# Layer 2's output projection: another order of features, tiles and PSUM banks

## The chip, the cores and the metric

The kernel runs on one core of a Trainium2 chip. The metric is the device time of one execution in microseconds. Three runs of the kernel before gave 1513.44 us in the median (1511.74 to 1513.91). The profile comes from one further execution.

## The reference, cut to what matters

A two-layer block with 512 latent tokens and 256 context tokens of width 1024. Each layer normalizes and modulates, mixes tokens in four branches of 256 features each, projects the 1024 mixed features with `w_out`, adds the result to x under a gate, normalizes again, and runs a convolutional FFN. In layer 2 only the latent tokens go on.

```python
def token_mixer(h_lat, h_ctx, ...):
    ya = gla_mixer(...)                       # gated linear attention, readout times silu(r)
    y = concatenate([ya, pool_mixer(zb), sgu_mixer(zc), conv_module(zd)]) @ w_out
...
x = layer_norm(ALPHA * x + m[2] * y, post_ln_w[l, 0], post_ln_b[l, 0])
h = modulate(x, m[3], m[4])
f = conv_ffn(h, ffn_w_up[l], ffn_conv_w[l], ffn_w_down[l])
x = layer_norm(ALPHA * x + m[5] * f, post_ln_w[l, 1], post_ln_b[l, 1])
```

## The kernel before, in words

All products are kept near fp32 accuracy by splitting each operand into a rounded part and a rest: `hi`/`lo` for weights, `hl`/`ll` for the latent tokens' features. `mm3` (lines 181 to 189) issues three matmuls per product: hi by hi, lo by hi, hi by lo. Line 133 is the subtraction that makes every rest (`lo`, `wl`, `ll`), on GpSimd or VectorE.

`mixers(l)` computes the four branches. At its end each of the eight feature blocks of 128 features is copied into `hl[k]` on ScalarE (line 865) and its rest into `ll[k]` (line 866, on VectorE for odd k, on GpSimd for even k), in the order `KORD`. Blocks 0 and 1 are the attention readout (`kT`, `qT`), 2 and 3 the pooled branch (`zs`), 4 and 5 the gated unit (`sy`, the tiles `cy`), 6 and 7 the convolution (`acc`).

What comes just before, in layer 2: the attention readout multiplies by the gate r on GpSimd (line 823), transposes on TensorE into a PSUM tile `yaT` (828), and ScalarE copies out with a scale (831). The convolution branch transposes its result into `cT` (799), normalizes it into `yn` (205 to 209), transposes back (805) and applies silu (810 to 813). The gated unit multiplies into a PSUM tile `s` (842), VectorE takes that out with bias and scale (846), and multiplies by the gelu of u (853); the gelu (499) reads the two columns `fl` that come last.

`out_proj` (lines 869 to 898) multiplies the blocks by `w_out`: each of four token tiles of 128 has two PSUM banks of 512 columns, y0 and y1. `w_out` comes in eight loads of 512 KB on SP's queue; the first two blocks of `KORD` get the weight buffers `hi`/`lo` that are free early, the other six lie in a pool of their own (`wh`, `wl`; line 882 and 133). Then `post_ln` (gate product 388, sum with the old x 389) and `norms` (two layer norms, lines 391 to 416) follow for a group of tiles, and `to_hT` (transposes `xT` 359, scale 365 and 367, copies 369) writes the new `hl`/`ll`. The constants of the norm (423, 424), the old x (384) and the gate rows `g` (435) are loaded into a pool whose memory the mixers' pools had. `ffn_up` then makes the first four FFN columns in two token halves, with the PSUM tiles `ul` in the banks 2, 3, 0, 5.

PSUM banks are handed out by rings, lists of bank numbers taken in turn (`rings`, `bank`). A bank is given on when every reader of its last tile is done. `stagger(ks, grp, n)` sets the loop order: all tiles of the group together over all but the last n blocks, then tile by tile over the last n.

The order in which an engine takes its instructions is not the program order: a planner, which simulates the timeline as the kernel is built, sorts each engine's queue by readiness and program order. On the chip each queue is taken in the order so fixed.

```python
def stagger(ks, grp, n):
    ks = list(ks)
    if ks[:-n]:
        yield ks[:-n], grp
    for t in grp:
        yield ks[-n:], (t,)
```

Of the kernel before, what the change touches and what calls it, by code (L numbers as in the profile page):

```python
# [13 lines left out]
ALU = mybir.AluOpType  # L14
# [5 lines left out]
KT = 8  # L20
# [30 lines left out]

CO, NCONST = offsets(CONSTS)
MO, NMIX = offsets(MIXW)
KORD = (0, 1, 6, 7, 2, 3, 4, 5)
PAIRS = ((0, 1), (3, 4), (2, 5))


# [1 line left out]
def kernel(  # L59
# [23 lines left out]
    V, S, G, PE = nc.vector, nc.scalar, nc.gpsimd, nc.tensor  # L83
# [11 lines left out]
    def rings(**kw):  # L95
        for n, r in kw.items():
            ring[n] = [r, 0]
# [344 lines left out]
# [8 lines that stand above are left out]
    def mixers(l, ms=None, pre=()):  # L450
        full = l == 0
# [214 lines left out]
        for p in range(2):  # L666
            V.scalar_tensor_tensor(out=sgb[:, p], in0=pt[:, p * 128:(p + 1) * 128], scalar=M["sgu_lnb"][:, p:p + 1],
                                   in1=M["sgu_b"][:, p * 128:(p + 1) * 128], op0=ALU.mult, op1=ALU.add)
# [27 lines left out]
        for t in order_t:  # L696
            po = bank("o", "sm")
            for c in range(2):
# [3 lines left out]
                for d in range(2):  # L702
                    i_s = st_of[d, ch]
                    if i_s == 0:
# [3 lines left out]
                                    in1=C["hm"].unsqueeze(2).to_broadcast([128, 4, 64]), op=ALU.mult)  # L708
# [60 lines left out]
        r_ = mx.tile([128, NT, 256], F32, name="r")  # L769
# [6 lines left out]
                V.scalar_tensor_tensor(out=r_[:, t], in0=r_[:, t], scalar=1.0, in1=pb[t][:, 0:256],  # L776
                                       op0=ALU.add, op1=ALU.mult)

        rings(**({"big": [2, 3], "sc": [4, 5]} if full else {"big": [4, 5], "sc": [0, 1]}))

        normalize([vg[:, t] for t in range(nt)], [vg[:, t] for t in range(nt)], "sgu", mx)

# [33 lines left out]
        for t0 in order_t[::2]:  # L816
            rs = rstd(ss[:, t0:t0 + 2].rearrange("p a b -> p (a b)"), 8, "rsg", 1.0 / 64.0, mx)
            yr = mx.tile([128, 2, 256], F32, tag="yr", name="yr")
            for i in range(2):
                V.tensor_tensor(out=yr[:, i].rearrange("p (h e) -> p h e", h=4),  # L820
                                in0=o_[t0 + i].rearrange("p (h e) -> p h e", h=4),
                                in1=rs[:, 4 * i:4 * i + 4].unsqueeze(2).to_broadcast([128, 4, 64]), op=ALU.mult)
            G.tensor_tensor(out=yr, in0=yr, in1=r_[:, t0:t0 + 2], op=ALU.mult)
            pt = bank("yaT", "sm")
            for k in range(2):
                for i in range(2):
                    o = k * 256 + i * 128
                    PE.transpose(pt[:, o:o + 128], yr[:, i, k * 128:(k + 1) * 128], ident)
            for k in range(2):
                ya = (kT, qT)[k][:, t0 * 128:(t0 + 2) * 128]  # L830
                S.activation(out=ya, in_=pt[:, k * 256:(k + 1) * 256], func=AF.Copy, scale=half[:, 0, k:k + 1])
# [25 lines left out]
        ys = [(kT, 0, LAT), (qT, 0, LAT), (zs[0], ZPAD, zo), (zs[1], ZPAD, zo), (sy[0], 0, LAT), (sy[1], 0, LAT),  # L857
              (yc[0], 0, CCTX), (yc[1], 0, CCTX)]
        for t0, n in spans:
            for k in KORD:  # L860
                y, o0, o1 = ys[k]
                o = o1 if t0 else o0
                src = y[:, o:o + n * 128]
                hi, lo = hcol(k, t0, n)
                S.activation(out=hi, in_=src, func=AF.Copy)
                sub_lo(V if k % 2 else G, lo, src, hi)
        es.close()

    def out_proj(l, groups, pb):
        with tc.tile_pool(name=f"ln1_{l}", bufs=2) as work, \  # L870
                tc.tile_pool(name=f"wo{l}", bufs=1, side="right") as wres:
            rings(sm=[6, 7] if l else [0, 1])
            ws = {}
            for i, k in enumerate(KORD):
                src = w_out[l, k * 128:(k + 1) * 128, :]
                if i < 2:
                    ws[k] = load_w(src, D)
                    continue
                st = load_st(src, D)
                hi = wres.tile([128, D], F32R, name=f"wh{k}")  # L880
                lo = wres.tile([128, D], F32R, name=f"wl{k}")
                S.activation(out=hi, in_=st, func=AF.Copy)
                sub_lo(V if k % 2 else G, lo, st, hi)
                ws[k] = (hi, lo)
            w, b = ln_consts(l, 0, work)
            gates = gate_get(l, 0, work)
            for grp in groups:
                ps = {t: (bank("y0", pb[t][0]), bank("y1", pb[t][1])) for t in grp}
                for ks, tiles in stagger(KORD, grp, KT):
                    for k in ks:  # L890
                        hi, lo = ws[k]
                        for t in tiles:
                            xh, xl = hcol(k, t)
                            for h in range(2):
                                s = slice(h * 512, (h + 1) * 512)
                                mm3(ps[t][h], hi[:, s], lo[:, s], xh, xl, k == KORD[0], k == KORD[-1], False)
                for _ in post_ln(l, 0, grp, ps, work, gates, w, b, lambda t: src_x(l, t), modT[l, 1]):
                    pass
# [233 lines left out]
    for l in range(DEPTH):  # L1132
# [3 lines left out]
        if l == 0:  # L1136
            out_proj(l, [(0, 1), (4, 5), (2,), (3,)], {0: (2, 3), 1: (4, 5), 4: (6, 7), 5: (2, 3), 2: (4, 5), 3: (6, 7)})
        else:
            out_proj(l, [(0, 1), (2,), (3,)], [(1, 4), (2, 3), (0, 5), (1, 4)])
        with tc.tile_pool(name=f"gT{l}", bufs=1, side="right") as gp, ExitStack() as late:  # L1140
            gT = [gp.tile([128, TOK if l == 0 else LAT], F32, name=f"gT{i}") for i in range(NF)]
            with ExitStack() as es:
# [151 lines left out]
```

## Time and profile before

| what | value |
|---|---|
| median of three runs | 1513.44 us (1511.74 to 1513.91) |
| profiled execution, its own time | 1510.28 us |
| span of its instructions | 1508.5 us |
| TensorE (PE) busy | 1448.1 us, 96% |
| VectorE (DVE) busy | 1172.2 us, 78% |
| ScalarE (ACT) busy | 544.7 us, 36% |
| GpSimd (POOL) busy | 830.0 us, 55% |
| mean granted TensorE clock | 0.989 |

Times in the rows are microseconds from the start of the span; a row with x8 stands for eight instructions run together. The time in brackets is how long the engine sat idle before, with the instruction that ended the wait. Matmuls overlap with their successors, so the distance of two starts, not the duration of one, is the pace. The execution profiled was 3.16 us faster than the median.

### The profile page before, as it was taken

The page shows a single profiled execution, that of the slowest core. Times are in us where ns is not written, and L with a number is a line of the kernel's source. Part 1 is how long each engine was busy: PE and PEld are TensorE (multiplying, and loading weights), DVE is VectorE, ACT ScalarE, POOL GpSimd, SP SyncE. Part 2 cuts the span into 40 slices and gives each one's busy share as a digit, 9 for nine tenths or more (in the row PEclk, how much of TensorE's full clock was granted, in tenths as well). Part 3 has the DMA queues.
Part 4 walks back from the last instruction along what each step waited for, and adds up shares of the span by engine and source line. Part 5 has one row for each costly group of instructions (what it writes and reads, how often), then busy time and mean ns, then how long its engine had stood idle before and what let it go on. Part 6 is the DMA issues. An engine that isn't in the chain of part 4 may idle for free.

```text
span 1508.5 us, 22357 instructions
## 1 busy us (share of the span) xinstructions
PE 1448.1 (96%) x8389; PEld 1185.7 (79%) x8389; DVE 1172.2 (78%) x1896; ACT 544.7 (36%) x936; POOL 830.0 (55%) x695
## 2 busy tenths in 40 slices
PE   6999999999999989999999989999899999999997
PEld 5776567788788878888888767986678888888875
DVE  6429987796988888787533699798687999889596
ACT  5443224245333322323211234254426454443121
POOL 2432635455665655543445597215466888777374
PEclk9999999999999999999999999999999999999999
DMA  9544410634877666521432366632162333333431
GB/s 377 195 165 158 140 54 15 228 135 159 313 266 240 239 215 216 178 70 56 165 100 85 116 204 239 209 125 71 58 234 72 98 98 98 98 98 93 173 112 56
DMA packets 67196, 227.11 MB, mean 151 GB/s; under 512 B 7289, under 2 KB 7945, under 8 KB 66065
## 3 DMA queue, kind: packets, MB, share of 16 engines
q1 hardware_dynamic: 67088, 225.69, 44.3%
q8 instruction: 66, 1.08, 0.3%
q14 instruction: 42, 0.34, 0.1%
HBM read 198.12 MB, written 27.55 MB: 150 GB/s over the span
## 4 chain that ended last, share of the span: by engine, by line
PE 62%; DVE 14%; DMA 12%; POOL 6%; issue 4%; ACT 2%; SPq 1%; POOLq 0%; DVEq 0%; ACTq 0%
PE ul L183 8%; PE ul L184 8%; PE ul L185 8%; PE f L187 5%; PE f L188 5%; PE f L189 5%; DMA ms<-in_wmodT 3%; POOL lo L133 2%; PE fl L183 2%; PE fl L185 2%; PE fl L184 2%; DVE acc L730 2%; DMA wl_f<-ms 2%; POOL ms L133 2%; PE tk L187 2%
## 5 line engine op out<-in xcount | busy, mean ns | idle before, releaser
L133 POOL TENSOR_TENSOR lo<-st,hi 128x512 fp32r<-128x512 f32 x300 | 412.2, 1397 | 228.0 <-ACT hi L147 175.1
L945 DVE SCALAR_TENSOR_TENSOR acc<-ul,cvw,acc 128x441 f32<-128x441 f32 (+2 forms) x660 | 437.1, 690 | 43.4 <-ACT acc L916 20.6
L147 ACT ACTIVATE hi<-st 128x1024 fp32r<-128x1024 f32 (+1 forms) x176 | 184.6, 1051 | 366.1 <-PE f L189 164.1
L184 PE MATMUL ul<-ll,hi 128*128 128x512 f32 (+1 forms) x768 | 286.4, 374 | 0.7 <-POOL ll L133 0.4
L183 PE MATMUL ul<-hl,hi 128*128 128x512 f32 (+1 forms) x768 | 284.8, 375 | 1.1 <-ACT hl L369 1.1
L185 PE MATMUL ul<-hl,lo 128*128 128x512 f32 (+1 forms) x768 | 285.4, 373 | 0.0
L187 PE MATMUL f<-hi,gh 128*128 128x512 f32 x440 | 171.8, 395 | 1.2 <-DVE gh L1007 1.2
L188 PE MATMUL f<-lo,gh 128*128 128x512 f32 x440 | 172.6, 394 | 0.0
L189 PE MATMUL f<-hi,gl 128*128 128x512 f32 x440 | 164.3, 396 | 6.4 <-POOL gl L133 5.3
L183 PEld LDWEIGHTS ul<-hl,hi 128*128 128x128 f32 x768 | 144.5, 190 | 28.3 <-issue 2.5
L185 PEld LDWEIGHTS ul<-hl,lo 128*128 128x128 f32 x768 | 145.5, 189 | 25.7 <-issue 0.4
L184 PEld LDWEIGHTS ul<-ll,hi 128*128 128x128 f32 x768 | 145.7, 190 | 24.6 <-POOL ll L133 0.7
L949 POOL TENSOR_TENSOR gT<-acc 128x768 f32<-128x768 f32 (+1 forms) x44 | 69.8, 1586 | 96.1 <-ACT acc L948 76.0
L730 DVE SCALAR_TENSOR_TENSOR acc<-cy,cmw,acc 128x798 f32<-128x798 f32 (+1 forms) x120 | 117.0, 1016 | 0.8
L183 PE MATMUL uc<-hc,hi 128*128 128x256 f32 x352 | 100.6, 286 | 6.5 <-DVE acc L945 6.4
L189 PEld LDWEIGHTS f<-hi,gl 128*128 128x128 f32 x440 | 82.6, 189 | 27.1 <-POOL gl L133 7.7
L185 PE MATMUL uc<-hc,lo 128*128 128x256 f32 x352 | 100.4, 285 | 0.0
L184 PE MATMUL uc<-lc,hi 128*128 128x256 f32 x352 | 100.4, 285 | 0.0
L187 PEld LDWEIGHTS f<-hi,gh 128*128 128x128 f32 x440 | 83.3, 189 | 20.6 <-issue 1.8
L188 PEld LDWEIGHTS f<-lo,gh 128*128 128x128 f32 x440 | 83.2, 189 | 18.3
L1007 DVE CAST gh<-gT 128x256 fp32r<-128x256 f32 x66 | 37.4, 572 | 64.9 <-PE f L188 64.9
L133 POOL TENSOR_TENSOR gl<-gT,gh 128x256 fp32r<-128x256 f32 x66 | 54.8, 833 | 57.8 <-DVE gh L1007 50.7
(304 smaller groups left out, 2843.6 us busy)
## 6 DMA issues: line engine op xcount, KB each, us to landing
st<-in_w_up SPq DMA_DIRECT2D x88, 512.0 KB, 3.5
st<-in_w_down SPq DMA_DIRECT2D x66, 512.0 KB, 3.5
ms<-in_wmodR SPq DMA_DIRECT2D x48, 512.0 KB, 4.1
ms<-in_wmodT SPq DMA_DIRECT2D x32, 512.0 KB, 3.7
ms<-in_wmod SPq DMA_DIRECT2D x8, 1024.0 KB, 12.3
st<-in_w_out SPq DMA_DIRECT2D x16, 512.0 KB, 3.5
x<-z SPq DMA_DIRECT2D x16, 512.0 KB, 2.8
z<-x SPq DMA_DIRECT2D x14, 512.0 KB, 8.8
```

Source lines behind the costliest of these rows:

```text
L133: eng.tensor_tensor(out=lo, in0=src, in1=f(hi), op=ALU.subtract)
L147: S.activation(out=hi[:, :n], in_=st[:, :n], func=AF.Copy)
L183: PE.matmul(ps, wh, xh, start=first, stop=False)
L184: PE.matmul(ps, wh, xl, start=False, stop=False)
L185: PE.matmul(ps, wl, xh, start=False, stop=last)
L187: PE.matmul(ps, xh, wh, start=first, stop=False)
L188: PE.matmul(ps, xh, wl, start=False, stop=False)
L189: PE.matmul(ps, xl, wh, start=False, stop=last)
L730: V.scalar_tensor_tensor(out=acc[i][:, :cw], in0=src, scalar=wj, in1=acc[i][:, :cw], op0=ALU.mult, op1=ALU.add)
L945: V.scalar_tensor_tensor(out=d, in0=u, scalar=w, in1=d, op0=ALU.mult, op1=ALU.add)
L949: G.tensor_tensor(out=gT[i][:, :n], in0=ag[:, :n], in1=aa[:, :n], op=ALU.mult)
L1007: V.tensor_copy(out=gh, in_=src)
```

## The change

Only layer 2's order changes, but for one table that now has an entry per layer:

- The blocks are copied and multiplied in the order 2, 3, 4, 5, 6, 7, 0, 1 in layer 2 (layer 1 keeps 0, 1, 6, 7, 2, 3, 4, 5). So `w_out`'s blocks are loaded in that order too, and 2 and 3 get the early buffers.
- `stagger` gets 4 instead of 8 in layer 2: tiles 0 and 1 together over the first four blocks, then tile 0, then tile 1 over the last four.
- The tiles' banks in layer 2 become (2,3), (4,5), (0,1), (2,3) instead of (1,4), (2,3), (0,5), (1,4).
- Behind the last token projection of layer 2, the ring `sm` shrinks to banks 6 and 7 (it had 6, 7, 2, 3): the two `yaT` and the two `s` take 6, 7, 6, 7.
- The attention readout's gate product in layer 2 runs on VectorE instead of GpSimd.

```diff
--- before.py
+++ after.py
@@ -51,7 +51,7 @@
 
 CO, NCONST = offsets(CONSTS)
 MO, NMIX = offsets(MIXW)
-KORD = (0, 1, 6, 7, 2, 3, 4, 5)
+KORDS = ((0, 1, 6, 7, 2, 3, 4, 5), (2, 3, 4, 5, 6, 7, 0, 1))
 PAIRS = ((0, 1), (3, 4), (2, 5))
 
 
@@ -776,7 +776,7 @@
                 V.scalar_tensor_tensor(out=r_[:, t], in0=r_[:, t], scalar=1.0, in1=pb[t][:, 0:256],
                                        op0=ALU.add, op1=ALU.mult)
 
-        rings(**({"big": [2, 3], "sc": [4, 5]} if full else {"big": [4, 5], "sc": [0, 1]}))
+        rings(**({"big": [2, 3], "sc": [4, 5]} if full else {"big": [4, 5], "sc": [0, 1], "sm": [6, 7]}))
 
         normalize([vg[:, t] for t in range(nt)], [vg[:, t] for t in range(nt)], "sgu", mx)
 
@@ -820,7 +820,7 @@
                 V.tensor_tensor(out=yr[:, i].rearrange("p (h e) -> p h e", h=4),
                                 in0=o_[t0 + i].rearrange("p (h e) -> p h e", h=4),
                                 in1=rs[:, 4 * i:4 * i + 4].unsqueeze(2).to_broadcast([128, 4, 64]), op=ALU.mult)
-            G.tensor_tensor(out=yr, in0=yr, in1=r_[:, t0:t0 + 2], op=ALU.mult)
+            (G if full else V).tensor_tensor(out=yr, in0=yr, in1=r_[:, t0:t0 + 2], op=ALU.mult)
             pt = bank("yaT", "sm")
             for k in range(2):
                 for i in range(2):
@@ -857,7 +857,7 @@
         ys = [(kT, 0, LAT), (qT, 0, LAT), (zs[0], ZPAD, zo), (zs[1], ZPAD, zo), (sy[0], 0, LAT), (sy[1], 0, LAT),
               (yc[0], 0, CCTX), (yc[1], 0, CCTX)]
         for t0, n in spans:
-            for k in KORD:
+            for k in KORDS[l]:
                 y, o0, o1 = ys[k]
                 o = o1 if t0 else o0
                 src = y[:, o:o + n * 128]
@@ -870,7 +870,7 @@
         with tc.tile_pool(name=f"ln1_{l}", bufs=2) as work, \
                 tc.tile_pool(name=f"wo{l}", bufs=1, side="right") as wres:
             rings(sm=[6, 7] if l else [0, 1])
-            ws = {}
+            ws, KORD = {}, KORDS[l]
             for i, k in enumerate(KORD):
                 src = w_out[l, k * 128:(k + 1) * 128, :]
                 if i < 2:
@@ -886,7 +886,7 @@
             gates = gate_get(l, 0, work)
             for grp in groups:
                 ps = {t: (bank("y0", pb[t][0]), bank("y1", pb[t][1])) for t in grp}
-                for ks, tiles in stagger(KORD, grp, KT):
+                for ks, tiles in stagger(KORD, grp, 4 if l else KT):
                     for k in ks:
                         hi, lo = ws[k]
                         for t in tiles:
@@ -1136,7 +1136,7 @@
         if l == 0:
             out_proj(l, [(0, 1), (4, 5), (2,), (3,)], {0: (2, 3), 1: (4, 5), 4: (6, 7), 5: (2, 3), 2: (4, 5), 3: (6, 7)})
         else:
-            out_proj(l, [(0, 1), (2,), (3,)], [(1, 4), (2, 3), (0, 5), (1, 4)])
+            out_proj(l, [(0, 1), (2,), (3,)], [(2, 3), (4, 5), (0, 1), (2, 3)])
         with tc.tile_pool(name=f"gT{l}", bufs=1, side="right") as gp, ExitStack() as late:
             gT = [gp.tile([128, TOK if l == 0 else LAT], F32, name=f"gT{i}") for i in range(NF)]
             with ExitStack() as es:
```

## Rows read from the trace of the kernel before

**Rows 1.** Stretches: from:to, length, then busy us (xcount) per engine, clock, DMA share, GB/s

```profile
1077.00:1090.00 13.00, 8.86 (x41) 6.91 (x42) 11.42 (x18) 7.60 (x13) 8.57 (x6) 1.00 0.22 74
...
1101.66:1144.00 42.34, 40.32 (x227) 34.24 (x226) 39.01 (x80) 16.45 (x30) 27.21 (x30) 1.00 0.44 160
...
1128.00:1147.00 19.00, 15.64 (x119) 13.91 (x117) 16.52 (x41) 11.87 (x30) 10.24 (x16) 1.00 0.14 58
...
1147.00:1480.00 333.00, 331.92 (x1511) 276.53 (x1511) 293.25 (x416) 131.90 (x183) 248.25 (x194) 1.00 0.33 105
```

**Rows 2.** TensorE in order of time: start, us, operation, [idle before, releaser]

```profile
1067.04 1.10 PE L842 MATMUL s<-mw,vg 128*64 128x128 f32 x16
...
1077.19 0.66 PE L828 MATMUL yaT<-cst,yr 128*128 128x128 f32 x4 [0.42 <-POOL yr L823]
...
1079.89 0.50 PE L187 MATMUL y<-hi,hl 128*128 128x512 f32 x1 [2.05 <-ACT hl L865]
...
1081.84 0.60 PE L805 MATMUL cT<-cst,yn 128*128 128x128 f32 x4
...
1089.36 0.50 PE L187 MATMUL y<-wh,hl 128*128 128x512 f32 x1 [1.91 <-ACT hl L865]
...
1126.93 0.39 PE L188 MATMUL y<-wl,hl 128*128 128x512 f32 x1
...
1127.16 0.39 PE L189 MATMUL y<-wh,ll 128*128 128x512 f32 x1
```

**Rows 3.** TensorE in order of time, start of layer 2's FFN

```profile
1128.98 0.74 PE L183 MATMUL ul<-hl,hi 128*128 128x256 f32 x4 [0.78 <-ACT hl L369]
...
1146.91 0.74 PE L183 MATMUL ul<-hl,hi 128*128 128x256 f32 x4 [0.32 <-ACT hl L369]
```

**Rows 4.** Chain of waits, 1070 to 1160 us: start, us, what

```profile
1092.50 0.33 SPq L423
...
1092.88 6.68 DMA lnb<-in_post_b
```

**Rows 5.** VectorE in order of time, 1044 to 1160 us

```profile
1076.01 0.54 DVE L810 TENSOR_SCALAR acc<-cT,half 128x256 f32<-128x256 f32 x1 [1.44 <-PE cT L805]
...
1077.14 0.73 DVE L846 SCALAR_TENSOR_TENSOR cy<-s,mw,sgb 128x512 f32<-128x512 f32 x1
...
1080.38 1.00 DVE L209 TENSOR_SCALAR yn<-cT,bmv_cm,rs_cm 128x256 f32<-128x256 f32 x2 [0.59 <-POOL rs_cm L194]
...
1083.52 2.61 DVE L133 TENSOR_TENSOR wl<-st,wh 128x1024 fp32r<-128x1024 f32 x1 [0.29 <-ACT wh L882]
...
1086.05 2.59 DVE L813 SCALAR_TENSOR_TENSOR acc<-yn,acc 128x256 f32<-128x256 f32 x1
...
1091.66 0.69 DVE L133 TENSOR_TENSOR ll<-acc,hl 128x512 fp32r<-128x512 f32 x1 [0.70 <-ACT hl L865]
...
1101.66 1.36 DVE L388 TENSOR_TENSOR y<-y,g 128x512 f32<-128x512 f32 x2 [4.48 <-DMA g<-gates]
...
1115.61 0.69 DVE L216 BATCH_NORM_STATS2 bst_m<-z 128x6 f32<-128x512 f32 x1 [1.17 <-POOL z L405]
```

**Rows 6.** GpSimd in order of time, 1044 to 1160 us

```profile
1064.89 1.27 POOL L133 TENSOR_TENSOR ll<-z,hl 128x512 fp32r<-128x512 f32 x1 [6.42 <-ACT hl L865]
...
1075.86 1.27 POOL L823 TENSOR_TENSOR yr<-yr,r 128x512 f32<-128x512 f32 x1
```

**Rows 7.** ScalarE in order of time, 1044 to 1160 us

```profile
1074.46 0.58 ACT L499 ACTIVATE tmp<-fl 128x512 f32<-128x512 f32 x1
...
1078.25 0.47 ACT L831 ACTIVATE qT<-yaT,half 128x256 f32<-128x256 f32 x1
...
1081.47 2.95 ACT L882 ACTIVATE wh<-st 128x1024 fp32r<-128x1024 f32 x3 [0.59 <-DVE yn L209]
```

**Rows 8.** TensorE in order of time, 870 to 886 us

```profile
880.31 1.74 PE L189 MATMUL f<-hi,gl 128*128 128x512 f32 x4 [3.01 <-POOL gl L133]
```

**Rows 9.** Stretch behind that pause, columns as in the first group

```profile
880.30:884.00 3.70, 3.69 (x10) 2.91 (x11) 3.70 (x7) 0.00 (x0) 3.70 (x5) 0.56 0.97 343
```

## The prediction

> **What bounds the kernel now.** I read the stretches first. From 1147 us on, TensorE works 331.92 of 333.00 us [rows 1]: whatever layer 2's FFN starts earlier or later by goes straight into the total. The change sits just ahead of it, so the question is what sets that start. Next TensorE in order of time: behind the mixers it pauses 0.42 us for GpSimd's gated product, 2.05 us for the first `hl` copy and 1.91 us for the copy of convolution feature 6, then streams `y` matmuls 0.23 us apart until about 1127.4 [rows 2]. Pauses: 4.4 us. If TensorE alone set the end, that would be the gain.
>
> It does not. The chain of waits leaves TensorE at 1092.50 and goes through SP's load of the layer norm's constants [rows 4]. These loads have memory that the mixers' pool gives back, and they go out 0.15 us after the pool's last reader, the `ll` copy of feature 7, 1091.66 + 0.69 [rows 5]. Behind them come the old x and the gate rows `g`; VectorE sits 4.48 us until `g` lands and starts the first post norm at 1101.66 [rows 5]. From there to 1144 VectorE works 39.01 of 42.34 us [rows 1]: it is the bound of the four post norms. TensorE has slack behind it: 3.36 us idle between 1128 and 1147 [rows 1], and the second token half of the first FFN columns waits for the last `hl` copies until 1146.91 [rows 3]. So the path is: convolution branch, pool release at 1092.4, constants and gates by DMA, VectorE's post norms, FFN. TensorE's three pauses lie beside it.
>
> **The change part by part.**
>
> *Order 2,3,4,5,6,7,0,1, tiles 0 and 1 together over the first four, banks (2,3) and (4,5).* The work stays 192 `y` matmuls, some 44 us at 0.23. Pooled features 2 and 3 are ready early: their copies run from about 1064 (the `ll` of the first at 1064.89 [rows 6]), and their weights take the two early slots that 0 and 1 had, with the same eight 512 KB loads in the same places of SP's queue. Banks 4 and 5 fall free with the second gelu, 1074.46 + 0.58 [rows 7]. So 24 matmuls (two features, two tiles, two halves, three products), 5.6 us, can stand where TensorE now waits; features 4 and 5 give 24 more, whose weights cannot start before 1081.47 [rows 7]. Both long pauses should go: 4.0 us of TensorE. On the path this is worth nothing by itself, since the first post norm still waits for `g`. Tile 0 then needs 72 matmuls and the last weights; from 1077.4 (the end of `yaT`, less its 0.42 us pause) that is 1094, with the twelve to twenty-four of tile 2 that fill in 1097 to 1100, still before 1101.66. If that cover were gone, each later microsecond would count in full.
>
> *What tiles 2 and 3 give.* Their `y` ends about 4.4 us earlier, at 1123 instead of 1127.4. VectorE can then fill pauses of its chain with their evacuations: it idles 42.34 - 39.01 = 3.33 us in the stretch [rows 1], 1.17 of it in one wait for GpSimd's end of tile 0's norm [rows 5]. Bounds 0 and 3.3; I take the middle, 1.6, because some of these waits are short round trips to GpSimd that no other tile's work fits into. Tile 3's third feature also frees the early weight buffers sooner, so GpSimd's split of the third and fourth FFN weight comes earlier too; same work, another place.
>
> *`sm` banks 6 and 7.* The second `yaT` and the second `s` now both use bank 7. Today the second half of `s` stands in front of the conv transposes on TensorE and its evacuation L846 (0.73 us at 1077.14) in front of the conv statistics' end on VectorE [rows 5]. Afterwards `s` must wait until ScalarE has emptied `yaT`, now 1078.25 + 0.47 [rows 7]. If the planner lets the conv branch pass, L846 (0.73), the product behind it (about the 0.69 of the `ll` copy of the same shape [rows 5]) and half of the 1.10 us of sixteen `s` matmuls [rows 2] leave the path: up to 2.0 earlier. If L846 keeps its place, it waits for `s`: the product ends 1.9 earlier (below), so bank 7 is free at 1076.8, `s` ends at 1077.9, and with a hand-over it costs 1.2.
>
> *Gating on VectorE.* Twice a 1.27 us GpSimd product [rows 6] becomes a VectorE product of the size of that 0.69 us copy. The one that matters can run from 1074.6, inside VectorE's 1.44 us pause before 1076.01 [rows 5]; so nothing is paid, and `yaT` comes up to 1.9 us earlier (1077.13 against 1075.25). Without that cover it costs 0.7. A row warns here: a VectorE product beside GpSimd's work took 2.61 us at 1083.52, and a 128x256 one behind it 2.59 [rows 5]; at twice the 0.69 us it would still end at 1076.0, when the pause ends.
>
> Together these two move the pool release by between -1.2 (later) and +2.0; I take +1.0, nearer the gain, because VectorE takes its queue in the planner's order and the conv statistics stand earlier in the program than the wait of `s` ends.
>
> *Tile 3 in banks 2 and 3.* These are the FFN's first two `ul` banks; today they are tile 1's and long free. The first columns now wait for tile 3's evacuation. The columns in banks 0 and 5 can go meanwhile, and the evacuation must come anyway before tile 3's norm; cost 0, up to 1 if TensorE's queue has the blocked ones in front.
>
> *Sum.* 1.0 (release) + 1.6 (filled pauses) + 0 (rest) = 2.6 us, all carried through the FFN. Against the profiled execution, span 1508.5 in 1510.28, this gives 1507.7; that execution lies 3.2 under the median of 1513.44, so the median becomes **1510.8 us**.
>
> *The clock.* TensorE's pause before the FFN grows from 0.78 us [rows 3] to about 4. Once it paused 3.01 us [rows 8], and the next 3.70 us show a granted clock of 0.56, near the 1.2 GHz level, and ten matmuls [rows 9], which at 0.23 take 2.3: a loss of 1.4, inside the 3.36 of slack. The Trainium skill, "TensorE: Matmul & The Clock Gate", section "HAM oscillation — how this bites in real kernels", says that matmuls which come in short bursts between waits start cold again each time. The rows agree for one pause; no row here shows a series. By the row the sum stays; by the page the first `ul` matmuls, which come in bursts as the `hl` copies land, would all run at half rate, and the slack would be used up.
>
> **Rivals.**
>
> 1. *Given back whole.* The release stays at 1092.4 and the pauses of VectorE are round trips; TensorE's 4 us become a longer wait before 1129, perhaps with the slow clock in it. For it: VectorE is 92% busy from 1101.66 [rows 1]. Against: the conv branch has two movable items. Gain 0 to 0.6: 1513.1 (1512.8 to 1513.5).
> 2. *Larger.* The conv branch also gets in front of the weight split on VectorE: the 2.61 us at 1083.52 [rows 5] leave the path on top. For it: that order is the planner's and hangs on a microsecond. Against: the weights start at the same event, the last `yn`. 1510.8 - 2.6 = 1508.2 (1506 to 1509).
> 3. *Slower: `y` in front of the conv transposes.* TensorE takes its queue in order. The last `cT` transposes stand at 1081.84, today behind eight `y` matmuls [rows 2]. If more than (1081.84 - 1077.4) / 0.23 = 19 stand in front, each further one delays the conv branch, the release and all behind it by 0.23. With the 24 of features 2 and 3 and eight of feature 4 it is 32, thirteen too many: 3.0 us; with all of feature 4, 3.9. Less the 1.6 of filled pauses: 1.4 to 2.3 slower, **1515.3** (1514 to 1517.5, the upper end with the bank wait of L846). For it: `y` work is now ready 4 us before the transposes. Against: the transposes come first in the program, and the planner knows when they are ready.
>
> **How the numbers follow.** Forecast (1509 to 1512.8) 0.38; rival 1 0.20; rival 2 0.20; rival 3 0.22. Two in a thousand, 3.0 us, is about what a measurement here can tell: faster means under 1510.4, slower over 1516.5. Faster: rival 2 and somewhat under half of the forecast, 0.20 + 0.17 = 0.37. Slower: half of rival 3, 0.11. Same: the rest, 0.52. The range leaves out the lower end of rival 2 and the upper part of rival 3: 1507 to 1515.5.
>
> **What would show it.** Right: no pause over 0.5 us on TensorE between 1077 and the last `y`; `y` ending 4 us earlier; the SP load of L423 about 1 us earlier; L388's first start near 1100.7; a pause of some 4 us before the first `ul`; the first wait-free `ul` second half near 1144.3. Rival 3 shows as more than 19 `y` matmuls in front of the last four `cT` transposes. The prediction is wrong in its root if the first L388 waits for TensorE instead of `g`, or if the FFN's start follows the end of `y` rather than VectorE.

## Result, and the profile after

The change made the kernel slower: 1520.29 us in the median of five runs (1516.03 to 1521.96) against 1513.44 us for the kernel before (five runs, 1509.80 to 1513.91), 6.85 us between the medians. The ratio between the runs is 1.0053, with an interval of 1.0035 to 1.007, which is 8 us. The time lies outside the predicted range and on the other side of no change.

The profiled execution after took 1521.96 us, 11.7 more than the one before, and not all of that is the change. The same kernel's executions differ by some microseconds in layer 1, ahead of anything edited. I therefore count every time below from one event ahead of the change, the first gelu of `vg` on ScalarE, and call the start of the first full-width `ul` matmul of layer 2's FFN **F**. From F to the end of the span lie 349.4 to 349.6 us in the profiles of all 20 kernels told of here, so what the change does to the time is what it does to F. In order: start, us, operation. Before:

```profile
1049.02 0.38 ACT L773 ACTIVATE vg<-tk 128x256 f32<-128x256 f32 x1 [0.97 <-PE tk L189]
...
1158.95 0.40 PE L183 MATMUL ul<-hl,hi 128*128 128x512 f32 x1
```

After:

```profile
1053.50 0.38 ACT L773 ACTIVATE vg<-tk 128x256 f32<-128x256 f32 x1 [0.97 <-PE tk L189]
...
1170.66 0.40 PE L183 MATMUL ul<-hl,hi 128*128 128x512 f32 x1
```

F is 109.93 before and 117.16 after. So 4.48 us of the 11.7 lie ahead of the change, and 7.23 us are its own, in line with the timed 8.

**Where they were lost first: the release.** TensorE after, in order of time, around what answers to [rows 2] and [rows 3]:

```profile
1083.91 1.09 PE L842 MATMUL s<-mw,vg 128*64 128x128 f32 x16
1084.94 0.66 PE L828 MATMUL yaT<-cst,yr 128*128 128x128 f32 x4
1085.43 0.60 PE L805 MATMUL cT<-cst,yn 128*128 128x128 f32 x4
...
1087.36 1.09 PE L842 MATMUL s<-mw,vg 128*64 128x128 f32 x16
1089.66 0.50 PE L187 MATMUL y<-wh,hl 128*128 128x512 f32 x1 [1.22 <-ACT wh L882]
...
1092.61 0.50 PE L188 MATMUL y<-wl,hl 128*128 128x512 f32 x1 [1.52 <-POOL wl L133]
...
1132.32 0.44 PE L359 MATMUL xT<-cst,xh 128*128 128x128 f32 x2 [2.19 <-DVE xh L412]
...
1139.93 1.54 PE L359 MATMUL xT<-cst,xh 128*128 128x128 f32 x6 [7.17 <-DVE xh L412]
1142.28 1.22 PE L183 MATMUL ul<-hl,hi 128*128 128x256 f32 x4 [0.81 <-ACT hl L369]
```

Both `s` come late: the first starts at 30.41 (before 18.02), and the second stands behind the second `yaT`, whose bank 7 it takes over, and ends at 34.95 (before 27.74). ScalarE and SP after:

```profile
1086.00 0.47 ACT L831 ACTIVATE qT<-yaT,half 128x256 f32<-128x256 f32 x1
...
1087.85 0.63 ACT L865 ACTIVATE hl<-cy 128x512 fp32r<-128x512 f32 x1
1088.56 2.95 ACT L882 ACTIVATE wh<-st 128x1024 fp32r<-128x1024 f32 x3
...
1120.39 1.06 ACT L147 ACTIVATE hi<-st 128x1024 fp32r<-128x1024 f32 x1 [3.28 <-PE y L189]
```

```profile
1099.43 0.33 SPq L423 DMA_DIRECT2D lnw<-in_post_w  x1
```

SP's load of `lnw`, at 43.48 before [rows 4], goes out at 45.93. The release is 2.45 late. The conversion of the late `w_out` blocks starts 0.11 behind the end of the second `s`, at 35.06; before, it started behind the last `yn` ([rows 7], 1081.47), at 32.45. But ScalarE was busy with copies until 0.08 before it, and VectorE, which takes the last steps to the release, did not stand waiting for its result. What changed there is VectorE's order. VectorE before, beside [rows 5]:

```profile
1068.18 0.75 DVE L846 SCALAR_TENSOR_TENSOR cy<-s,mw,sgb 128x512 f32<-128x512 f32 x1
...
1078.73 0.66 DVE L853 TENSOR_TENSOR cy<-cy,tmp 128x512 f32<-128x512 f32 x1
```

and after:

```profile
1084.27 0.99 DVE L209 TENSOR_SCALAR yn<-cT,bmv_cm,rs_cm 128x256 f32<-128x256 f32 x2 [0.25 <-POOL rs_cm L194]
1085.18 0.74 DVE L846 SCALAR_TENSOR_TENSOR cy<-s,mw,sgb 128x512 f32<-128x512 f32 x1
...
1086.53 0.68 DVE L853 TENSOR_TENSOR cy<-cy,tmp 128x512 f32<-128x512 f32 x1
1087.54 1.36 DVE L133 TENSOR_TENSOR ll<-qT,hl 128x512 fp32r<-128x512 f32 x1 [0.33 <-ACT hl L865]
...
1090.71 0.73 DVE L846 SCALAR_TENSOR_TENSOR cy<-s,mw,sgb 128x512 f32<-128x512 f32 x1
1091.47 1.63 DVE L853 TENSOR_TENSOR cy<-cy,tmp 128x512 f32<-128x512 f32 x1
1093.03 3.42 DVE L133 TENSOR_TENSOR wl<-st,wh 128x1024 fp32r<-128x1024 f32 x1
...
1098.58 0.69 DVE L133 TENSOR_TENSOR ll<-acc,hl 128x512 fp32r<-128x512 f32 x1
```

The last `yn` itself ends at 31.76, earlier than before (32.36). But before, VectorE had emptied both `s` (L846) and made both products (L853) ahead of it; after, all four stand behind it, 3.78 us together, on the way to the last reader of the pool, the `ll` at 1098.58. From 1087.54 to there VectorE never pauses longer than 0.10 us. This is read from the order of one profile; what the edits do to it one by one is told below.

**Where they were lost next: GpSimd's queue.** VectorE after, answering to [rows 5]:

```profile
1082.98 0.69 DVE L823 TENSOR_TENSOR yr<-yr,r 128x512 f32<-128x512 f32 x1
...
1108.63 1.34 DVE L388 TENSOR_TENSOR y<-y,g 128x512 f32<-128x512 f32 x2 [2.67 <-DMA g<-gates]
...
1123.47 0.69 DVE L216 BATCH_NORM_STATS2 bst_m<-z 128x6 f32<-128x512 f32 x1 [1.18 <-POOL z L405]
...
1126.40 2.20 DVE L402 SCALAR_TENSOR_TENSOR z<-z,rs_p,lnb 128x832 f32<-128x832 f32 x1
...
1132.65 1.07 DVE L402 SCALAR_TENSOR_TENSOR z<-z,rs_p,lnb 128x832 f32<-128x832 f32 x1
...
1139.34 0.54 DVE L412 TENSOR_SCALAR xh<-z,bmv_m,rs_m 128x512 f32<-128x512 f32 x1
```

The first post norm still waits for `g`, and starts 2.49 late, as the release does. But tile 1's `xh` (1139.34) is at 85.84 instead of 77.51, 8.3 late. One reason is GpSimd, here before (`z` L405 is the end of a tile's post norm, `lo` the split of an FFN weight, `rs` a power that closes a statistic):

```profile
1108.50 5.05 POOL L133 TENSOR_TENSOR lo<-st,hi 128x512 fp32r<-128x512 f32 x4 [1.27 <-DMA st<-in_w_up]
...
1117.02 0.80 POOL L405 TENSOR_TENSOR z<-z,lnw 128x192 f32<-128x192 f32 x1 [0.94 <-ACT z L401]
1117.90 0.60 POOL L405 TENSOR_TENSOR z<-z,lnb 128x192 f32<-128x192 f32 x1
...
1119.91 5.22 POOL L133 TENSOR_TENSOR lo<-st,hi 128x512 fp32r<-128x512 f32 x4
```

and after:

```profile
1115.47 5.94 POOL L133 TENSOR_TENSOR lo<-st,hi 128x512 fp32r<-128x512 f32 x4 [0.83 <-ACT hi L147]
...
1123.91 5.84 POOL L133 TENSOR_TENSOR lo<-st,hi 128x512 fp32r<-128x512 f32 x4
1129.71 0.59 POOL L405 TENSOR_TENSOR z<-z,lnw 128x192 f32<-128x192 f32 x1
...
1132.09 0.62 POOL L405 TENSOR_TENSOR z<-z,lnb 128x192 f32<-128x192 f32 x1
...
1138.11 0.55 POOL L194 TENSOR_TENSOR rs_m<-rs_m,nhalf 128x1 f32<-128x1 f32 x1 [3.27 <-DVE rs_m L193]
```

Tile 1's end of norm stood in front of the second group of `lo`; now it stands behind it. Tile 3's earlier `y` over blocks 2 and 3 frees the weight buffers (the third `hi`, 1120.39, waits for a `y`), so this group is ready earlier and was sorted in front. The chain of waits in the profile after goes through this group, and behind it through VectorE's work on the first post norms of tiles 2 and 3. TensorE then waits 2.19 and 7.17 us for `xh`. Stretches of after, columns as in [rows 1]:

```profile
1108.63:1150.97 42.34, 32.06 (x152) 26.69 (x151) 38.04 (x75) 14.37 (x25) 27.63 (x28) 0.84 0.46 166
1132.50:1151.50 19.00, 10.90 (x63) 9.97 (x63) 16.32 (x39) 9.01 (x20) 9.90 (x13) 0.64 0.21 86
```

The second one answers to 1128:1147 before: 10.90 us of TensorE work instead of 15.64, at a granted clock of 0.64 instead of 1.00. VectorE's busy time in the 42.34 us from the first post norm is 38.04 instead of 39.01: no pause was filled.

The step from the late `xh` to F can be added up. From the first `ul` to F, before and after:

```profile
1128.98:1158.95 29.97, 27.38 (x216) 25.86 (x217) 20.62 (x51) 18.93 (x44) 15.01 (x22) 1.00 0.10 37
```

```profile
1142.28:1170.66 28.38, 28.26 (x217) 27.97 (x217) 13.90 (x34) 16.53 (x42) 12.08 (x18) 0.90 0.05 19
```

The first `ul` is 8.82 late. TensorE's idle time behind it shrinks from 2.59 to 0.12, which gives 2.47 back, and the same matmuls take 28.26 us at a granted clock of 0.90 instead of 27.38 at 1.00, which adds 0.88: together 7.23.

### The profile page after: what moved, and what is told of

It reads as the page before. It is cut to its first block, busy times and chain, and to the rows that moved or that the text cites. A ratio compares the mean times of both kernels' runs of the same rounds, so it can differ in the third digit from the quotient of the medians.

```text
span 1520.1 us, 22362 instructions
## 1 busy us (share of the span) xinstructions
PE 1452.6 (96%) x8389; PEld 1190.1 (78%) x8389; DVE 1176.8 (77%) x1898; ACT 545.6 (36%) x936; POOL 829.1 (55%) x693
## 4 chain that ended last, share of the span: by engine, by line
PE 72%; DVE 12%; DMA 7%; POOL 5%; issue 3%; ACT 1%; SPq 0%; POOLq 0%; DVEq 0%; ACTq 0%
PE ul L183 10%; PE ul L184 9%; PE ul L185 9%; PE f L187 5%; PE f L189 5%; PE f L188 5%; PE uc L183 2%; PE uc L184 2%; PE uc L185 2%; PE fl L183 2%; PE fl L185 2%; PE fl L184 2%; POOL lo L133 2%; PE tk L187 2%; PE tk L189 2%
```

## The experiments

All figures are in us from the first gelu of `vg`; release is SP's load of `lnw`; the ratio is to the kernel before on the same chip (five rounds), with its interval. F, release and `xh` come from one profile per kernel.

| kernel | edits left in | release | tile 1's xh | F | ratio |
|---|---|---|---|---|---|
| before | none | 43.48 | 77.51 | 109.93 | 1 |
| after | all five | 45.93 | 85.84 | 117.16 | 1.0053 [1.0035, 1.007] |
| e1_ring | all but the ring | 45.29 | 85.21 | 114.62 | 1.0021 [1.0003, 1.0038] |
| e4_gate | all but the gating | 46.84 | 86.16 | 116.36 | 1.0033 [1.0018, 1.0048] |
| e2_pool | all, split held on GpSimd | 45.91 | 80.94 | 113.91 | 1.0014 [0.9997, 1.0031] |
| e3_dve | all, tiles 2, 3 held on VectorE | 45.88 | 80.22 | 119.49 | 1.0055 [1.0036, 1.0074] |
| e6_ring_pool | e1 and e2 together | 45.30 | 78.63 | 113.33 | 1.0027 [1.0016, 1.0038] |
| f1_first | all, s ahead of yaT | 47.33 | 81.79 | 115.10 | 1.0035 [1.0021, 1.0048] |
| fg_all | all, s ahead, y and split held | 46.64 | 79.93 | 118.08 | 1.0053 [1.0037, 1.0069] |
| b1_pool | none, split held | 43.47 | 75.71 | 110.61 | 1.0017 [1.0004, 1.003] |
| m1_mix | ring, gating | 45.49 | 85.37 | 119.31 | 1.0051 [1.0032, 1.0069] |
| m2_order | order, pairing, banks | 45.57 | 84.09 | 113.87 | 1.0023 [1.001, 1.0036] |
| m3_order_pool | the same, split held | 45.58 | 78.68 | 113.16 | 1.0032 [1.0017, 1.0047] |
| h1_behind | as m2, y held | 43.46 | 73.15 | 111.80 | 1.0007 [0.9995, 1.0019] |
| r1_ring | ring | 45.22 | 83.11 | 115.51 | 1.0038 [1.0021, 1.0056] |
| r2_gate | gating | 45.66 | 79.57 | 111.96 | 1.0011 [1.0003, 1.002] |
| r3_banks | banks | 43.48 | 76.78 | 108.83 | 1.0009 [0.9997, 1.002] |
| r4_kord | order, pairing | 45.57 | 84.23 | 115.76 | 1.0045 [1.0033, 1.0057] |
| v2_held | order, pairing, y held | 43.49 | 77.03 | 110.21 | 1.0015 [1.0001, 1.0028] |
| v4_held_banks | the same, banks, split held | 43.48 | 76.73 | 115.19 | 1.0035 [1.002, 1.0051] |

F less that of before and the timed loss agree within 2.5 us everywhere; smaller differences between two kernels I don't read.

**GpSimd's order alone (e2_pool).** On the changed kernel the split of the third and fourth FFN weight is put behind tile 1's last power; the release is untouched. `tc.issue_after(x)` has the planner place what stands under it behind the instruction x. The edits here and below are cut to layer 2.

```diff
-        wts = [load(ct) for ct in first]
+        wts = [load(ct) for ct in first[:2]]
+        with tc.issue_after(held["norm1"]):     # layer 2: last rs power of tile 1's norm, on GpSimd
+            wts += [load(ct) for ct in first[2:]]
```

> The changed kernel with one more order: on GpSimd, the four subtractions that split the third and fourth FFN weight may not stand ahead of the last power of tile 1's second norm. Nothing else is told to the planner. Theory queue: tile 1's xh comes 5 to 6 us earlier (85.8 to about 80 us behind the first gelu of v), the first ul matmul moves as much (88.8 to about 83), the first full-width ul matmul from 117.2 to about 112 to 113; time about 1515.5. Theory VectorE order (evacuations of tiles 2 and 3 stand in front of tile 1's norm because their y is ready earlier): xh of tile 1 stays within 1 us of 85.8, time 1519 to 1520. Theory bank: the release stays at 45.9 in any case.

GpSimd of this kernel (its lines are numbered 4 to 6 higher), and below TensorE's waits from 1095 to 1175 us (waited for, us in total, times, longest):

```profile
1121.78 0.80 POOL L409 TENSOR_TENSOR z<-z,lnw 128x192 f32<-128x192 f32 x1 [2.13 <-ACT z L405]
...
1123.52 0.55 POOL L194 TENSOR_TENSOR rs_m<-rs_m,nhalf 128x1 f32<-128x1 f32 x1 [0.26 <-DVE rs_m L193]
...
1127.84 5.12 POOL L133 TENSOR_TENSOR lo<-st,hi 128x512 fp32r<-128x512 f32 x4
```

```profile
PE xT L363 <- DVE xh L418: 5.7, 1, 5.7
```

Tile 1's `xh` came 4.9 earlier, the wait fell from 9.4 to 5.7, F by 3.25, and the ratio from 1.0053 to 1.0014, with intervals that do not meet. So in the changed kernel the place of this split carries about 3 of the 7.23; tile 2's `xh` paid part of it back (92.32 against 86.89). In kernels with the old ring the same edit gains no time (e6 and m3 below).

**The ring, the gating, and VectorE's order (e1_ring, e4_gate, e3_dve).**

```diff
-  ... "sc": [0, 1], "sm": [6, 7]}))                       # e1: as before
+  ... "sc": [0, 1]}))
-  (G if full else V).tensor_tensor(out=yr, ...)           # e4: as before
+  G.tensor_tensor(out=yr, ...)
+  with tc.issue_after(held["xh1"]):                       # e3: post norms of tiles 2 and 3
+      for _ in post_ln(...): pass
```

> The changed kernel with one part undone: the ring for the readout and the gated unit keeps banks 6, 7, 2, 3, so the second s no longer waits for the second yaT in bank 7. Changed kernel: 1520.3 us; the load of the norm's constants 45.9 us after the first gelu of v, 43.5 in the kernel before. Theory bank (the late s holds the mixers' inner pool, whose memory the late w_out weights get): the first late weight conversion returns from 35.1 to about 32.5 us behind that gelu, the load of the constants to about 43.5, time about 1517.9. Theory queue (GpSimd's weight splits stand in front of tile 1's norm): the release may move, but 4 to 5 us of the loss stay, time 1517 to 1519. If neither: 1520 or more.

> The changed kernel with the readout's gate product back on GpSimd. Theory bank: the second yaT comes later by the difference of 1.27 and 0.69 us, so s, the inner pool and the release do too: 0.5 us slower, 1520.8. Theory that VectorE's added 0.7 us is what delays the convolution branch: 0.7 us faster or more, 1519.5. Neither touches tile 1's norm; a change of over 2 us would mean that the planner's order turned over elsewhere.

> The changed kernel with one more order: on VectorE, nothing of the first post norm of tiles 2 and 3 may stand ahead of tile 1's xh. Theory VectorE order: xh of tile 1 moves 4 us or more earlier (85.8 to under 82 behind the first gelu of v), first ul likewise, time 1515 to 1516. Theory queue: VectorE then only waits for GpSimd at the same places, xh of tile 1 moves by under 2 us unless GpSimd's order changes with it, and the last xh gets later, so 1519 to 1522.

With the old ring `s` ends at 29.39, but 2.5 of 7.23 are all that returns: the last `cT` transposes, now behind 24 `y` matmuls, come at 34.05 instead of 32.82, and the release is only 0.64 earlier. With gating back on GpSimd the release is 0.9 later and F 0.8 earlier, within what differs anyway. Holding tiles 2 and 3 on VectorE brings tile 1's `xh` 5.6 forward, as far as the held split does, so it was late by VectorE's order too; but the last `xh` goes 4.7 back (100.0) and the time stays: VectorE has no room to give.

**Mending two or three things at once (e6_ring_pool, f1_first, fg_all, b1_pool).** f1 puts the code of `s` in front of that of `yaT`; fg_all also holds `y` behind the last conv transposes (edit shown below) and the split as in e2; b1 is e2's edit on the kernel before.

> The changed kernel with the old ring of banks (6, 7, 2, 3 for yaT and s) and GpSimd's split of the third and fourth FFN weight behind tile 1's norm: both earlier edits together. Theory (two causes that add): release 45.1 as with the ring alone, tile 1's xh at 75 to 78, first full ul at 111.5 to 113.5 (after: 117.2; ring alone 114.6, queue alone 113.9), ratio to before 1.0000 to 1.0018. Rival (one cause seen twice: the ring alone gained by moving the split in GpSimd's queue): first full ul 113.5 to 114.5, no better than either alone, ratio 1.0014 to 1.002.

> The changed kernel with the gating products s put in front of the readout yaT in program order, so that s takes banks 6 and 7 before yaT does; the ring itself stays as changed. Theory: s no longer waits for the second yaT (ends before 29.5 instead of 34.95), but the conv transposes then stand behind about 20 y matmuls as they did with the old ring (last cT near 33.5-34), so the release comes at 44.5 to 45.2 instead of 45.9; the first full ul at 114 to 116 instead of 117.2; ratio to before 1.002 to 1.0035, as with the old ring. Rival (the shared bank is the whole loss): release at 43.5, first full ul at 110 to 112, ratio 0.9995 to 1.001. Rival (the bank does not matter): release 45.9, ratio 1.0045 to 1.006.

> The changed kernel with s in front of yaT in program order, the y matmuls of layer 2 on TensorE behind the last conv transposes, and GpSimd's split of the third and fourth FFN weight behind tile 1's norm. Theory: the release goes back to 42.8 to 43.6 (before 43.5, after 45.9), tile 1's xh comes at 74 to 77, and the y of tiles 2 and 3 are still done by 77, so the first full ul comes at 108.5 to 110.5 (before 109.9, after 117.2); ratio to before 0.9985 to 1.0005. Rival (the early y matmuls of several tiles cost the FFN's start by themselves, by GpSimd's and VectorE's queue order, whatever the release): release at 43.5 but the first full ul at 112 or later, ratio 1.0012 or more.

> The kernel before, with GpSimd's split of the third and fourth FFN weight held behind the last power of the second token tile's norm. Times are counted from the first gelu of v. Theory (two causes: a later release of the mixers' memory, and the place of that split in GpSimd's queue): in the kernel before, tile 1's norm already stands in front of the split, only one small power behind it, so little is to be had: tile 1's xh from 77.5 to 75-76.5, the last tile's xh at 94.4 within 0.7, the first full ul at 109.9 within 0.8, ratio to before 0.9990 to 1.0008. Rival (the order of GpSimd's queue costs time in either kernel, and the change only inherited it): the first full ul 2 to 3 us earlier, ratio 0.998 to 0.9985. Rival (the later weight pays it back): 1 to 2 us later, ratio 1.001.

e6 gains 1.3 in F over e1, but not in time: the two repairs do not add. In f1 `s` is early (29.82), but the second `yaT` slips to 35.99 and the release gets later still. fg_all missed: TensorE stood 4.85 us in front of the second `yaT`, waiting for the gating product, which VectorE now had behind the conv branch. b1 brings tile 1's `xh` 1.8 forward and tile 2's 2.3 back and is a little slower (1.0017, 1.0004 to 1.003), outside what was expected: the kernel before had no such loss to mend, since only tile 1's last power stood behind the split there (1125.10).

**The two halves (m1_mix, m2_order, m3_order_pool, h1_behind).** m1 is the kernel before with ring and gating, m2 with order, pairing and banks; m3 adds e2's edit to m2, and h1 this to m2:

```diff
+  with tc.issue_after(held["cT2"]):          # layer 2: the last transpose back of the conv branch
       mm3(ps[t][h], hi[:, s], lo[:, s], xh, xl, ...)
```

> The mixers' part of the change alone, on the kernel before: banks 6 and 7 for yaT and s, gating on VectorE; feature order, banks of the token tiles and pairing as before. Times are counted from the first gelu of v. Theory A (the shared bank delays the release, and the rest of the loss comes from GpSimd's order, which the y order brings): s ends at 33 to 35 (before 27.7), release 44 to 46 (before 43.5, after 45.9); GpSimd's order stays as before, so nothing is added: first full ul at 110.5 to 112.5 (before 109.9, after 117.2), ratio 1.0003 to 1.0018. Theory B (the mixers' part is the whole loss): first full ul 115 or later, ratio 1.0035 or more. Theory C (it gains, as the prediction had it): release 42.5, ratio 0.999.

> The output projection's part of the change alone: feature order, pairing over four features and the banks of the token tiles as changed; bank ring and gating of the mixers as before. Theory A: some twenty y matmuls stand in front of the last conv transposes (last cT at 33.5 to 34.5, before 32.8), release 44.2 to 45.3, and two of GpSimd's four late splits stand in front of tile 1's norm, so tile 1's xh comes at 80 to 84; first full ul at 113 to 116, ratio 1.002 to 1.004. Theory B (mixers' part is the whole loss): first full ul at 109 to 111, ratio 0.999 to 1.0007.

> The output projection's part alone as in the run beside it, and GpSimd's split of the third and fourth FFN weight behind tile 1's norm. Theory A (queue order and release add): the release as there, tile 1's xh 3 to 5 earlier (76 to 79), first full ul 1.5 to 3 earlier (111 to 113), ratio 1.0005 to 1.0025. Rival (the queue order does not matter once the mixers are as before): no difference to the run beside it.

> The output projection's part alone, and its y matmuls on TensorE behind the last conv transposes. That leaves the mixers and the release as before, and in this order GpSimd has tile 1's norm in front of the late split without further holding. Theory A: last cT at 32.8, release 43.2 to 43.8, tile 1's xh 75 to 78, the last tile's xh 93 to 95.5, first full ul at 108.5 to 110.5; ratio 0.9988 to 1.0006: the loss is gone, and the features' order gains nothing. Theory B (the early y of tiles 2 and 3 fill VectorE's pauses, worth 1.6 as the prediction had it): first full ul at 107 to 108.5, ratio 0.9985. Theory C (the order costs the FFN's start by itself): first full ul 112 or later, ratio 1.0012 or more.

The mixers' half alone costs as much as the whole change, the other half about half of it; they don't add. For h1 no loss can be measured (1.0007, 0.9995 to 1.0019), but its interval meets that of m2, and its F, 2.07 under m2's, missed the expected 108.5 to 110.5. The first theory for m3 is out: tile 1's `xh` comes 5.4 earlier than in m2 and the time does not follow, since tile 2's comes 5.8 later. So with the old mixers the place of the split decides little; h1, which has the old release again, points to the release without showing it.

**One edit alone (r1_ring, r2_gate, r3_banks, r4_kord),** each on the kernel before.

> On the kernel before, one edit alone: yaT and s in banks 6 and 7 only. Theory A (the shared bank is the mixers' loss): the second s waits for the copies of the second yaT and ends at 33 to 36 (before 27.7), the y matmuls stand behind it and begin near 35 (before 30.9), the first post norm at 55 to 59 (before 52.6); first full ul at 114 to 119 (before 109.9), ratio 1.0030 to 1.0055. Rival (the loss needs the gating on VectorE too): s ends by 30, first full ul at 112 or earlier, ratio below 1.0015.

> On the kernel before, one edit alone: the gating product of layer 2 on VectorE. Theory A (harmless without the shared bank): the second yaT comes up to 1.5 earlier than 28.2; 24 y matmuls stand in front of the last conv transposes instead of eight, so that these come at 33 to 34.5 instead of 32.8 and the release at 43.5 to 45; first full ul at 109.5 to 112, ratio 0.9995 to 1.0015. Rival (it costs by itself, by VectorE's queue): first full ul at 113 or later, ratio 1.002 or more.

> On the kernel before, one edit alone: the token tiles' banks (2,3), (4,5), (0,1), (2,3). The orders of TensorE and GpSimd stay as before. Theory A (tile 3 in the FFN's first banks costs 0 to 1): release 43.3 to 43.6, first full ul at 109.5 to 111, ratio 0.9993 to 1.0010. Rival (the banks are where the output projection's part loses): first full ul at 112 or later, ratio 1.0015 or more.

> On the kernel before, one edit alone: features in the order 2, 3, 4, 5, 6, 7, 0, 1 with tiles 0 and 1 together over the first four. Theory A (the order is the output projection's loss, by the conv transposes behind 24 y matmuls and by GpSimd's late split in front of tile 1's norm): last cT at 34 to 35.5, release 45 to 46, tile 1's xh at 81 or later, first full ul at 112.5 to 116, ratio 1.0015 to 1.004. Rival (the order is free, the loss is in the banks): first full ul at 111 or earlier, ratio below 1.0010.

r1: the shared bank delays `s` (34.55) and the release (by 1.74); the emptying and the product of the second `s` (1085.54 and 1086.31) stand behind the last `yn` on VectorE here too. With the old feature order no `y` goes before `s`; the first post norm then waits for TensorE, not for `g`. TensorE and VectorE of r1:

```profile
1082.46 1.97 PE L842 MATMUL s<-mw,vg 128*64 128x128 f32 x16 [0.29 <-ACT qT L831]
...
1105.50 1.30 DVE L388 TENSOR_TENSOR y<-y,g 128x512 f32<-128x512 f32 x2 [1.02 <-PE y L189]
```

r4 has the changed kernel's wait to a tenth without its mixers. The last conv transposes (first `vg` 1052.58, so 34.92), the release (45.57) and TensorE's waits of r4:

```profile
1087.50 0.60 PE L805 MATMUL cT<-cst,yn 128*128 128x128 f32 x4
```

```profile
1098.15 0.33 SPq L423 DMA_DIRECT2D lnw<-in_post_w  x1
```

```profile
PE xT L359 <- DVE xh L412: 9.5, 2, 7.2
```

So order and ring each cost 5 to 6 us of F alone, by the waits in different ways: the ring through late `y`; the order with a late release and the split ahead of tile 1's norm in GpSimd's queue, though m3, which has the banks as well, gained nothing by moving that split. Gating costs 0.5 to 3 us by its ratio (it lets 24 `y` in front of the last conv transposes, 35.67, and the first post norm waits for TensorE here too), the banks alone nothing that can be measured.

**Order kept, conv branch protected (v2_held, v4_held_banks).** v2 is r4 (m2 with the old banks) with the first feature's `y` held behind `yaT` and the others behind `cT2`; v4 has the new banks and e2's edit on top.

> The feature order and the pairing of the change with the mixers and the token tiles' banks of before; on TensorE the y of the first feature (12 matmuls) are held behind the last yaT transpose, those of all other features behind the last conv transposes. Theory A (TensorE's pause of 2 us is filled at no cost to the release): first y at 29, last cT at 32.1 to 32.8, release 43.3 to 43.6, last y at 77 to 78.5, tile 1's xh at 73 to 76, first full ul at 108 to 110 (before 109.9; with all y behind the conv transposes 111.8); ratio 0.9985 to 1.0003. Rival (the features' order has a cost left that is not the release): first full ul 111 or later, ratio 1.0010 or more.

> The same with the changed banks of the token tiles and with GpSimd's split of the third and fourth FFN weight behind tile 1's norm. Theory A: release 43.3 to 43.6, tile 1's xh at 73 to 76; the first ul columns wait for tile 3's evacuation out of banks 2 and 3 (about 1.0, as with all y behind the conv transposes), first full ul at 108.5 to 111; ratio 0.999 to 1.001. Rival: as beside it.

TensorE of v2 (first `vg` at 1049.97), and one of its stretches:

```profile
1082.02 0.91 PE L809 MATMUL cT<-cst,yn 128*128 128x128 f32 x4 [0.49 <-DVE yn L209]
...
1124.35 0.40 PE L189 MATMUL y<-wh,ll 128*128 128x512 f32 x1
...
1126.91 0.44 PE L363 MATMUL xT<-cst,xh 128*128 128x128 f32 x2 [2.17 <-DVE xh L416]
```

```profile
1102.03:1144.37 42.34, 39.05 (x207) 33.67 (x205) 36.80 (x79) 15.15 (x29) 27.34 (x30) 0.92 0.44 166
```

This is the change as it was meant: TensorE's two long pauses are gone, the last `y` is at 74.38 instead of 78.14, 3.8 earlier, the release is the old one (43.49). Against r4, from which only the holding differs, F falls from 115.76 to 110.21 and the ratio from 1.0045 to 1.0015, with intervals that do not meet. So what the order costs comes from where its `y` stand on TensorE; with them held, the release and GpSimd's order around tile 1's norm are as before, so these two are not told apart here. F is then 110.21 against 109.93 before, and the ratio, 1.0001 to 1.0028, lies above what was hoped for (0.9985 to 1.0003). TensorE's gain went into waits, 2.17 of it in one for VectorE's `xh`. v4, put at 108.5 to 111, missed: F 115.19. The release is as in v2, but tile 2's `xh` went from 88.34 to 93.97, and TensorE's first `ul` columns waited 2.4 for tile 3 to leave their banks; which of its two edits did it was not separated. No version beat the kernel before.

## Why the prediction was wrong, by its steps

- **TensorE's pauses lie beside the path, worth nothing by themselves: right.** v2_held removes the two long ones and gains nothing; it is rival 1 (0.20) as it was written, with TensorE's gain turned into a wait and a lower clock behind it. And the path named was the right one as far as the first post norm: it waits for `g`, and is late by what the release is late (2.49 and 2.45).
- **The release, put at 1.0 earlier (1.2 later to 2.0 earlier): wrong, and outside its bounds.** It is 2.45 later. The late end was worked out with `yaT` coming 1.9 earlier. It came 3.3 later (31.44 against 28.17): the last `o` ended 2.0 later, VectorE took the gating product behind the conv statistics, at 1082.98, and TensorE took the first `s`, itself late, in front of it. Bank 7 went on to the second `s` only then. So the emptying and the products of both `s` fell behind the last `yn` on VectorE, 3.78 us, where the late end had 1.2 for one of them (0.76 of it from its figures; no row prices the hand-over in the rest). r1 shows that the ring by itself delays `s` and the release; how the 2.45 divides among the edits, no run shows.
- **The step that failed most: "GpSimd's split of the third and fourth FFN weight comes earlier too; same work, another place", cost 0.** It is the same work, but in an in-order queue the place is the cost: 5.84 us in front of tile 1's end of norm. With it and the release TensorE's first `ul` came 8.8 late, and the slack in front of the FFN, which the prediction had at 3.36, was used up. Holding the split (e2_pool) gave 3.25 of F back, in the changed kernel; with the old ring it gave no time back.
- **VectorE's pauses, filled for 1.6: wrong.** The pauses stayed (38.04 busy of 42.34 after, 36.80 in v2_held, 39.01 before [rows 1]). The longest in v2_held, 2.42 and 1.67, wait for GpSimd's part of a norm (`z`, line 409 of that kernel, and `rs_m`); an earlier `y` of another tile filled none.
- **Rival 3, `y` in front of the conv transposes, 0.22: its mechanism is real, but not in the changed kernel.** Its sign came there: 24 `y` stand in front of the last four `cT`, more than the 19 allowed. But the `y` started at 23.33 instead of 30.87, and the last `cT` came at 31.93, 0.9 earlier than before. With the old ring it stands: 24 `y` in front, `cT` 1.2 to 2.1 late, the release 1.8 to 2.1 late (e1, m2, r4), and v2_held takes the loss away. The net price was too small, since 1.6 of gain was taken off and the split on GpSimd was not in it.
- **Banks of tile 3, 0 to 1: not contradicted** (r3: 1.0009, 0.9997 to 1.002). **Gating, 0, or 0.7 uncovered: too low**; r2 has 1.0011 (1.0003 to 1.002), 0.5 to 3 us.
- **The clock, a loss of 1.4 inside the slack: wrong about the slack.** The stretch in front of the FFN shows two waits and a granted clock of 0.64, where before had 1.00. The Trainium skill, "TensorE: Matmul & The Clock Gate", section "HAM oscillation — how this bites in real kernels", says that matmuls in short bursts between waits start cold again; the trace agrees with 0.64 here and 0.82 in 1126.90 to 1145.90 us of v2_held, behind a wait of 2.17. From the first `ul` to F the same matmuls took 0.88 us longer at a clock of 0.90, with 0.12 us of idle time left to take it up; that is an estimate of the clock's cost from two rows, as no run changed the clock alone.
- Of the signs named, none of the right ones came: pauses of 1.22 and 1.52 on TensorE ahead of the last `y`, `y` ending 1.9 earlier instead of 4, `lnw` later. Neither of the two signs of a wrong root came either; the loss lay between them, in the orders of two queues, VectorE's and GpSimd's, of which the argument had left the second at nothing.

What stays open: why the edits do not add. In F, order and ring cost 5.8 and 5.6 alone, the two halves 9.4 (m1) and 3.9 (m2), all five 7.2. Several delay the release, and each edit also re-sorted the queues of the other engines, so no run changes one delay and nothing else. Of the 7.23, e2_pool accounts for 3.25; the rest is argued from the waits.

## What to carry to other kernels

Where a planner fixes in-order queues, price an edit that makes work ready earlier by what it will be sorted in front of, on every engine, and not only by what it fills. A bank or buffer shared by two short stages is a wait chain: follow who holds the next memory down to the load that starts the next stage. And before filling an engine's pauses, ask whether the engine behind it can take the work earlier; here 3.8 us of TensorE bought nothing.

## What the runs showed of the hardware that was not expected

The same VectorE instruction, `z` L402 over 832 columns, took 2.20 us at 1126.40, beside GpSimd's split, and 1.07 at 1132.65, when GpSimd was between short steps. Four splits on GpSimd took 5.05 and 5.22 before and 5.94 and 5.84 after. Moving the split thus also moved which VectorE work stood beside it. No run changed this overlap alone, so that it is the cause is not shown.
